# A hybrid decoder step on one core: x handed over turned, block A projected without the tokens' norms, decode work first

## The chip, the core and the metric

The kernel runs on one core of one Trainium2 chip. The metric is the device time of one execution in microseconds (us), the median of several executions. Per-instruction times come from one profiled execution, whose own time stands beside the median below. The core has a matrix engine (PE, with weight loads shown as PEld), a vector engine (DVE), an activation engine (ACT), GpSimd (POOL), and SyncE (SP), which issues most of the DMA transfers.

## What is computed

One layer of a decoder trunk on 1024 prompt tokens and 32 sample tokens (8 sequences of 4), with 2048 features per token:

```python
def mixer_layer(x, pos, conv_buf, attn_fn, norm_in, w_in, g_q, g_k, g_kidx, w_conv, w_out):
    p = split_proj(rmsnorm(x, norm_in) @ w_in)      # 7760 columns
    q = partial_rope(rmsnorm(q, g_q), pos, ROPE_DIM)          # 8 heads x 128
    k = partial_rope(rmsnorm(k, g_k), pos, ROPE_DIM)          # 2 heads x 128
    qi = partial_rope(p["q_idx"], pos, IDX_ROPE_DIM)          # 16 index heads x 64
    ki = partial_rope(rmsnorm(p["k_idx"], g_kidx), ...)       # 64, and 16 head weights w_idx
    attn = attn_fn(q, k, v, qi, ki, wi)    # each query keeps its 256 best keys by
                                           # sum_h w[t,h] relu(q_idx[t,h] . k_idx[s])
    conv, new_buf = short_conv(p["c"] * p["h"], conv_buf, w_conv)
    mix = concat([attn * silu(p["z_attn"]), p["b"] * conv * silu(p["z_conv"])])
    return x + mix @ w_out, k, v, ki, new_buf
```

`rmsnorm(x, g)` divides each token by the root of its mean square and multiplies by `g`. The sample tokens search 8192 cached index keys in pages, and gather the 256 selected rows of the key and value caches. Besides y, the new k, v, index keys and convolution states are returned.

## The kernel before

**Tiling.** The work is cut into block A (prompt tokens 0 to 511 and the 32 sample tokens, 544 columns, kept as two halves of 288 and 256 columns) and block B (prompt tokens 512 to 1023, 512 columns). The projection keeps the features in the partitions: 16 k-tiles of 128 features. For each output tile of 128 columns of `w_in`, `proj` walks over four weight chunks; a chunk is one 256 KB transfer with the weights of four k-tiles (128x512). Both operands are split into a high and a low part: ACT casts `wh` (L494), DVE subtracts to get `wl` (L121, the line of the DVE helper). The same is done for x in `x_part`: ACT writes `xh` (L344), DVE writes `xl`. Each k-tile then costs three matmuls per half (`xh,wh`, `xl,wh`, `xh,wl`, L512).

**Stages.** Each block computes index queries `qi` (8 tiles), index keys `ki` (80 columns), k, v and q (`head_tiles`), the gate z (8 tiles) and the convolution (8 times 4 tiles, `conv_tiles(b, j)`), block A first. The output projections stand at the end. `w` has 4 buffers, `wl` and `wh` 3 each.

**Fillers.** Everything else runs as generators. `slot()`, called after each weight chunk, lets each of four pipes put some instructions into the stream: `main` (index scores and attention of the prompt tiles), `dec` (decode attention), `rms` (the norms of block B) and `vec` (the searches for the 256th best score). Generators in `later` are one-off tails such as `ki_rest`. A scheduler fixes the order of every engine at build; on the chip each engine executes its own list strictly in order. `hp` is the priority that chunk work has over fillers.

**x.** x arrives as rows (tokens in the partitions). `x_load`, `x_rstd` and `x_scale` load the rows, compute each token's factor and scale the rows. PE transposes 128x128 pieces into PSUM (`psx`), and `x_part` splits them from there. Before the first projection, `norm_in`, `w_conv` and `state_conv` are loaded as `rows` and turned by two PE transposes (`pr`). Block B is treated likewise: `x1_load`, `x1_scale` and `prep_x1`, the last of them called after each weight chunk of `conv_tiles(0, 7)`; tiles `xq` hold its rows and come from the pool `g4` of 6 buffers, which also holds the scores `acc` of the prompt search.

**Decode.** `decode_index` gathers index keys of the cache and scores them, `decode_select` searches (with the int16 tile `S`, 128x2304), turns the selection into row numbers (`way`, `pt`, `rid`), and `decode_attend` gathers and attends. In the kernel before `decode_index` and `decode_select` come behind `prompt_index` and `prompt_select` of tiles 2 and 3.

Of the kernel before, what the change touches and what calls it, by code (L numbers as in the profile page):

```python
# [8 lines left out]
F32 = mybir.dt.float32  # L9
# [104 lines left out]
def build(tc, ctx, I, O, stop=None):  # L114
# [86 lines left out]
    def w_out0(ch, c0, m):  # L201
        return I["w_out0"][c0 // 128, :, 4 * ch:4 * ch + 4]

    x_src = [(0, 128, xpr[256:384]), (256, 32, xsa), (128, 128, xpr[384:512]),
             (288, 128, xpr[0:128]), (416, 128, xpr[128:256])]
    x_raw = []

    def x_load(j):

        c0, n, src = x_src[j]  # L210
        if j == 0:
            big = gp.tile([128, 2304], F32, tag="sc", bufs=1, name="xsc")
# [63 lines left out]
    w_d = dp.tile([512], F32, name="w_d", tag="w_d")  # L276

# [57 lines left out]
    rx1 = const((128, 4), "rx1")  # L335

    def x_part(k, ps, xs, hi, lo, a, w):

        for c0, n, parts in xs:
            if a <= c0 < a + w:  # L340
                for a2, w2, t in parts:
                    if a2 <= 128 * k < a2 + w2:
                        transpose(ps[:, c0 - a:c0 - a + n], t[:n, 128 * k - a2:128 * k - a2 + 128], n)
        nc.scalar.activation(out=hi[:, a:a + w], in_=ps[:, :w], func=AF.Copy, scale=norm[:, k:k + 1])  # L344
        stt(lo[:, a:a + w], ps[:, :w], norm[:, k:k + 1], hi[:, a:a + w], MUL, SUB)
# [4 lines left out]
    def x_rstd(js, eng="av"):  # L350

        n = len(js)
        ss = sm((128, 2, n, 2), name="ssx")
        nc.vector.memset(ss, 0.0)
        for c, j in enumerate(js):
            _, rows_, parts = x_raw[j]
            for h, (a, w, t) in enumerate(parts):
                sqx = e2((128, 1024), BF, name="sqx")
                o = ss[:rows_, h % 2, c, h // 2:h // 2 + 1]
                if eng[h % 2] == "a":  # L360
                    nc.scalar.activation(out=sqx[:rows_, :w], in_=t[:rows_, :w], func=AF.Square, accum_out=o)
                else:
                    nc.vector.tensor_tensor_reduce(out=sqx[:rows_, :w], in0=t[:rows_, :w], in1=t[:rows_, :w], scale=1.0,
                                                   scalar=0.0, op0=MUL, op1=ADD, accum_out=o)
        v = sm((128, n), name="vx")
        tt(ss[:, 0], ss[:, 0], ss[:, 1], ADD)
        tt(v, ss[:, 0, :, 0], ss[:, 0, :, 1], ADD)
        ts(v, v, 1.0 / D, EPS, MUL, ADD)
        return rsqrt(v, n, "rx")

    def x_scale(j, h, r, c, eng=None):
        _, n, parts = x_raw[j]
        a, w, t = parts[h]
        if eng is nc.scalar:
            nc.scalar.activation(out=t[:n, :w], in_=t[:n, :w], func=AF.Copy, scale=r[:n, c:c + 1])
        else:
            (eng.tensor_scalar if eng else ts)(t[:n, :w], t[:n, :w], r[:n, c:c + 1], None, MUL)

    def prep_x0():

        x = x_tiles()

        def second():
            yield 1
            yield 1
            x_load(3)
            x_load(4)
            yield 1
            yield 1
            r = x_rstd((3, 4))  # L390
            for _ in range(4):
                yield 1
            for c, j in enumerate((3, 4)):
                for h in range(len(x_raw[j][2])):
                    x_scale(j, h, r, c)
            for _ in range(2):
                yield 1
            for k in range(KT):
                x_part(k, pj(name="psx"), x_raw, *x[k], 288, 256)
                yield 1  # L400
            hp[0] = 200

        r0, r1 = x_rstd((0, 1)), x_rstd((2,))
        for h in range(2):
            x_scale(0, h, r0, 0, nc.scalar)
            x_scale(1, h, r0, 1, nc.scalar)
            x_scale(2, h, r1, 0)
        pr = psm((128, 256), name="pr")
        transpose(pr[:, 0:128], rows[:, 0:128])
# [1209 lines left out]
```

## Time and profile before

| | us |
|---|---|
| median of 3 executions | 2209.12 (2206.09 to 2209.97) |
| the profiled execution | 2209.53 |
| its span, first to last instruction | 2207.6 |
| PE busy | 2162.5 (98%) |
| DVE busy | 1317.3 (60%) |
| ACT busy | 1088.3 (49%) |
| POOL busy | 480.5 (22%) |

Busy time is the union of an engine's instructions. A matmul's record is longer than its distance to the next one, because matmuls overlap in the pipeline; the distance of two starts in the timeline is the better price. The granted clock (PEclk) is 1.00 when PE has its full clock and 0.50 at half.

### The profile page before, as it was taken

What the parts mean: (1) busy time and instruction counts of PE and PEld (TensorE: products, weight loads), DVE (VectorE), ACT (ScalarE), POOL (GpSimd) and SP (SyncE); (2) the same over time, 40 slices, a digit from 0 to 9 for tenths busy, and PEclk for the clock granted to TensorE, in tenths of its full rate; (3) what the DMA queues carried; (4) which work ended last, traced back from release to release, by engine and by line L of the source; (5) the groups of instructions that cost most, each with busy time, mean ns of one, the idle gap of its engine ahead of it and who ended that gap; (6) DMA issues with size and microseconds to landing.
All of it is one profiled execution on the core that took longest, in us unless ns stands there. A gap on an engine that the chain in (4) does not pass through costs nothing.

```text
span 2207.6 us, 37829 instructions
## 1 busy us (share of the span) xinstructions
PE 2162.5 (98%) x13502; PEld 1941.8 (88%) x13502; DVE 1317.3 (60%) x2994; ACT 1088.3 (49%) x2112; POOL 480.5 (22%) x697
## 2 busy tenths in 40 slices
PE   6999999999999999999899999999999999999999
PEld 5899999999999999787688888888888899999887
DVE  6556666555555654799866666556667556443222
ACT  4346666334436566422257684445675565332221
POOL 2111011111113222142531143432331111210000
PEclk9999999999999999999999999999999999999999
DMA  5423444344344333333343344433343384448343
GB/s 195 131 90 117 125 138 135 118 141 131 123 144 140 118 116 104 107 117 113 102 134 117 117 150 129 118 122 105 113 128 113 102 301 117 123 119 275 134 134 110
DMA packets 203720, 290.81 MB, mean 132 GB/s; under 512 B 37588, under 2 KB 87948, under 8 KB 203404
## 3 DMA queue, kind: packets, MB, share of 16 engines
q1 hardware_dynamic: 192268, 254.83, 36.0%
q0 software_dynamic: 11264, 33.57, 5.5%
q8 instruction: 106, 1.74, 0.3%
q14 instruction: 82, 0.67, 0.1%
HBM read 247.53 MB, written 40.78 MB: 131 GB/s over the span
## 4 chain that ended last, share of the span: by engine, by line
PE 50%; DMA 0%; DVE 0%; issue 0%; POOL 0%
PE pj L512 33%; PE po L1503 8%; PE ix L855 1%; PE ix L854 1%; PE pt L174 1%; PE lg L1346 1%; PE dpo L1412 1%; PE kst L174 1%; PE sc L178 1%; PE sc L179 1%; PE po L179 1%; PE po L177 1%; PE po L178 1%; PE sc L177 1%; PE p L174 0%; PE pq L174 0%
## 5 line engine op out<-in xcount | busy, mean ns | idle before, releaser
L512 PE MATMUL pj<-xh,wl 128*128 128x288 f32 (+2 forms) x2800 | 793.0, 329 | 6.9 <-DVE wl L121 6.8
L512 PE MATMUL pj<-xh,wh 128*128 128x288 f32 (+2 forms) x2800 | 791.1, 328 | 6.9 <-DVE xl L121 2.7
L512 PE MATMUL pj<-xl,wh 128*128 128x288 f32 (+2 forms) x2800 | 796.1, 330 | 0.0
L121 DVE TENSOR_TENSOR wl<-w,wh 128x512 fp32r<-128x512 f32 (+1 forms) x613 | 444.1, 726 | 431.2 <-ACT wh L494 397.2
L494 ACT CAST wh<-w 128x512 fp32r<-128x512 f32 x616 | 379.2, 616 | 604.8 <-PE pj L512 380.0
L512 PEld LDWEIGHTS pj<-xh,wh 128*128 128x128 f32 (+1 forms) x2800 | 477.1, 189 | 51.8 <-DVE xl L121 3.1
L512 PEld LDWEIGHTS pj<-xh,wl 128*128 128x128 f32 (+1 forms) x2800 | 474.6, 189 | 51.6 <-DVE wl L121 11.2
L512 PEld LDWEIGHTS pj<-xl,wh 128*128 128x128 f32 (+1 forms) x2800 | 475.1, 189 | 42.2
L886 ACT ACTIVATE junk<-acc,se,se 128x512 int8<-128x512 f32 (+5 forms) x186 | 181.1, 974 | 27.4 <-DVE se L121 24.2
L1096 POOL DMA_INDIRECT G<-in_cache_kidx,gidx x64 | 64.3, 1004 | 388.6 <-PE gd L179 140.4
L121 DVE SCALAR_TENSOR_TENSOR acc<-ixr,wsg,acc 128x512 f32<-128x512 f32 (+3 forms) x150 | 98.3, 668 | 45.9 <-ACT ixr L857 44.7
L857 ACT ACTIVATE ixr<-ix,wab 128x512 f32<-128x512 f32 (+3 forms) x160 | 95.3, 613 | 54.9 <-PE ix L855 53.6
L512 PE MATMUL pj<-mxh,wl 128*128 128x272 f32 x512 | 109.8, 292 | 0.0
L512 PE MATMUL pj<-mxl,wh 128*128 128x272 f32 x512 | 109.4, 291 | 0.0
L512 PE MATMUL pj<-mxh,wh 128*128 128x272 f32 x512 | 108.9, 291 | 0.0
L1392 POOL DMA_INDIRECT Vs<-in_cache_v,rid x64 | 66.4, 1038 | 123.8 <-DVE Vl L121 36.1
L1004 ACT CAST pthl<-pt 128x256 fp32r<-128x256 f32 x144 | 49.6, 371 | 80.6 <-PE pt L174 79.4
L121 DVE TENSOR_TENSOR pthl<-pt,pthl 128x256 fp32r<-128x256 f32 x144 | 57.2, 420 | 50.6 <-ACT pthl L1004 50.0
L512 PEld LDWEIGHTS pj<-mxh,wh 128*128 128x128 f32 x512 | 81.5, 189 | 0.7
L512 PEld LDWEIGHTS pj<-mxl,wh 128*128 128x128 f32 x512 | 81.6, 189 | 0.3
L512 PEld LDWEIGHTS pj<-mxh,wl 128*128 128x128 f32 x512 | 81.3, 189 | 0.4
L990 POOL TENSOR_SCALAR P<-P,l 128x128 f32<-128x128 f32 (+7 forms) x64 | 51.9, 811 | 133.5 <-DVE l L989 102.7
(430 smaller groups left out, 3233.7 us busy)
## 6 DMA issues: line engine op xcount, KB each, us to landing
w<-in_w_in SPq DMA_DIRECT2D x480, 256.0 KB
w<-in_w_out SPq DMA_DIRECT2D x128, 256.0 KB
q_d<-qt SPq DMA_DIRECT2D x72, 64.0 KB
xr<-in_x_a SPq DMA_DIRECT2D x16, 272.0 KB
out_y_a<-xr SPq DMA_DIRECT2D x16, 272.0 KB
xq<-in_x_prompt SPq DMA_DIRECT2D x8, 512.0 KB
xq<-in_x_prompt SPq DMA_DIRECT2D x16, 256.0 KB
q<-q_d SPq DMA_DIRECT2D x32, 128.0 KB
```

Of the source, the lines that this page charges most:

```text
L121: i = f(*a, **k)
L174: nc.tensor.transpose(out, in_, ident[:p, :p])
L177: nc.tensor.matmul(out, lh, rh, start=start, stop=False)
L494: nc.scalar.copy(hi, w)
L512: nc.tensor.matmul(p[:m, :n], w[c][:, k % 4], x[k][b][:, a:a + n], start=(k == 0 and c == b), stop=(k == KT - 1 and c == 1))
L857: nc.scalar.activation(out=r[:, :w], in_=ps[:, :w], func=AF.Relu, scale=wab[:, g, h:h + 1])
L886: nc.scalar.activation(out=junk[:, :n], in_=S, func=AF.Sign, scale=sg, bias=cand, accum_out=s)
L990: nc.gpsimd.tensor_scalar(P[:, :n], P[:, :n], l, 0.5, MUL, MUL)
L1004: nc.scalar.copy(t[:, 0], ptv)
L1096: nc.gpsimd.indirect_dma_start(out=G, out_offset=None, in_=cki, in_offset=bass.IndirectOffsetOnAxis(ap=idx[:, 8 * s + g:8 * s + g + 1], ax ...
L1392: nc.gpsimd.indirect_dma_start(out=W[:, hf], out_offset=None, in_=cv, in_offset=bass.IndirectOffsetOnAxis(ap=rid[:, hf, q:q + 1], axis=0))
L1503: nc.tensor.matmul(ps[i], x[k_][b][:, 128 * i:128 * i + 128], w[c], start=(k_ == 0 and c == b), stop=(k_ == KT - 1 and c == 1))
```

## The change

The host hands x over turned (features in the partitions), as `x_a` and `x_b`, and also `norm_in`, `w_conv` and `state_conv`. `x_part` reads the loaded tile itself; the 144 `psx` and 2 `pr` transposes are gone. The first half of `x_a` is loaded in steps of 1, 1, 1, 1 and then 2 k-tiles, between the weight chunks of the first output tile; the second half in steps of 2 k-tiles per two slots.

Block A is projected from x without the tokens' factors. These come later, from 10 additional loads of the rows (`xt`) with an ACT square each: `rx`, and through DRAM as the rows `R` (factor of each token) and `R2` (its square). They are multiplied in where a result is used: in ki, k, v, the q norm (`mean`, through `ex`), the gate and the convolution (one or two more DVE products per piece). `ki_rest`, `k_rest` and `v_rest` wait with their remaining work for `rx`. Block B is still scaled ahead, but by one `tt` product of a tile with `R1` for each two k-tiles (8 of 128x1024) in place of 16 `ts` products with a column.

Decode goes first in its pipes, its queries are made separately, the last convolution of block A takes its weight columns in pairs (`group` 2), the early `wl` moves from POOL to DVE, and the scaling of the attention weights P by l moves from POOL to ACT. The area for the descriptors of POOL's DMAs is made smaller.

```diff
+        t = g4((128, n, w), name="xs") if n > 1 else g2((128, n, w), name="xs1")
+        nc.sync.dma_start(t, I["x_a"][:, k:k + n, cols])
...
-        nc.scalar.activation(out=hi[:, a:a + w], in_=ps[:, :w], func=AF.Copy, scale=norm[:, k:k + 1])
-        stt(lo[:, a:a + w], ps[:, :w], norm[:, k:k + 1], hi[:, a:a + w], MUL, SUB)
+        nc.scalar.activation(out=hi[:, a:a + w], in_=raw, func=AF.Copy, scale=norm[:, k:k + 1])
+        stt(lo[:, a:a + w], raw, norm[:, k:k + 1], hi[:, a:a + w], MUL, SUB)
...
+        for c in range(4):
+            if c < 3:
+                early.append(load_w(w_in(c, C_QI, 128)))
+            raw = []
+            for n in ((1, 1, 1, 1), (2, 2), (2, 2), (2, 2))[c]:
+                raw += x_load(0, 4 * c + len(raw), n)
+            for k in range(4):
+                put(0, 4 * c + k, raw[k])
...
+                    nc.sync.dma_start(t[rs], src[:, 1024 * h:1024 * h + 1024])
+                    sqx = e2((128, 1024), BF, name="sqx")
+                    nc.scalar.activation(out=sqx[rs], in_=t[rs], func=AF.Square, accum_out=ss[rs, i, h:h + 1])
...
+        while b == 0 and "rx" not in done:
+            yield 1
...
-        for i, (_, _, ((_, _, t),)) in enumerate(parts):
-            ts(t, t, rx1[:, i:i + 1], None, MUL)
+        for t in parts:
+            tt(t, t, R1[0].unsqueeze(1).to_broadcast([128, 2, 512]), MUL)
...
+            for p, c in nat(b, ps):
+                tt(out[:, c], p, R[:, c], MUL)
+            nc.scalar.activation(out=th, in_=out, func=AF.Tanh, scale=0.5)
+            stt(out, th, 1.0, out, ADD, MUL)
...
-        group = 1 if after is None or b == 0 else 2
+        group = 1 if after is None else 2
...
-                nc.scalar.copy(ce[:, c], p)
+                if b == 0:
+                    tt(ce[:, c], p, R2[:, c], MUL)
+                else:
+                    nc.scalar.copy(ce[:, c], p)
...
+            if b == 0:
+                tt(y, y, R, MUL)
...
-            nc.gpsimd.tensor_scalar(P[:, :n], P[:, :n], l, 0.5, MUL, MUL)
+            ts(l, l, 0.5, None, MUL)
+            nc.scalar.activation(out=P[:, :n], in_=P[:, :n], func=AF.Copy, scale=l)
...
-    main.add(prompt_index(2), prompt_index(3), decode_index())
+    main.add(decode_index(), prompt_index(2), prompt_index(3), decode_queries())
     main.add(*(prompt_attend(i) for i in range(4)))
-    vec.add(prompt_select(2), prompt_select(3), decode_select())
+    vec.add(decode_select(), prompt_select(2), prompt_select(3))
...
+    R1.append(g2(name="R1"))
+    nc.sync.dma_start(R1[0], r1_d.rearrange("(o n) -> o n", o=1).to_broadcast([128, 512]))
```

How the instructions stand is shown at three places. **First**, the start of PE's list, before:

```order
L174 MATMUL pr<-ident,rows 128x128 x2
L174 MATMUL psx<-ident,xsc 128x128 x5
L174 MATMUL psx<-ident,xs 128x32 x5
L174 MATMUL psx<-ident,xs 128x128 x5
L512 MATMUL pj<-xh,wh 128x288
L174 MATMUL psx<-ident,xsc 128x128
L174 MATMUL psx<-ident,xs 128x32
L174 MATMUL psx<-ident,xs 128x128
```

and after:

```order
L479 MATMUL pj<-xh,wh 128x288
L479 MATMUL pj<-xl,wh 128x288
L479 MATMUL pj<-xh,wl 128x288
L479 MATMUL pj<-xh,wh 128x288
L479 MATMUL pj<-xl,wh 128x288
L479 MATMUL pj<-xh,wl 128x288
```

The transposes ahead of the first matmuls and between them are gone. **Second**, DVE where block A's convolution ends and block B begins, before (`y` is the product of the last convolution, `xl` the low part of block B's x, `zt` belongs to the attention of a prompt tile, `se` to a search):

```order
L121 TENSOR_TENSOR y<-pj,y 128x288
L121 TENSOR_TENSOR pthl<-pt,pthl 128x256
L121 TENSOR_TENSOR y<-pj,y 128x256
L121 TENSOR_TENSOR wl<-w,wh 128x512
L121 TENSOR_SCALAR se<-tot,se_7576 128x1
L121 SCALAR_TENSOR_TENSOR se_7577<-se,se_7577 128x1
L121 TENSOR_TENSOR zt<-po,zt 128x256
L121 SCALAR_TENSOR_TENSOR xl<-psx,norm,xh 128x512 x3
L121 TENSOR_SCALAR se<-tot,se_7576 128x1
L121 TENSOR_TENSOR wl<-w,wh 128x512
L121 TENSOR_TENSOR wl<-w,wh 128x4x80
```

and after, the last reads of the convolution's PSUM tiles (`cm<-pj,R`) with what follows, and the rows ahead of the first `xl`:

```order
L121 TENSOR_TENSOR cm<-pj,R 128x288
L121 TENSOR_TENSOR cm<-pj,R 128x256
L121 TENSOR_TENSOR pthl<-pt,pthl 128x256
L121 TENSOR_TENSOR wl<-w,wh 128x4x80
L121 TENSOR_TENSOR S<-S 128x2304
...
L121 TENSOR_SCALAR pt_10531<-pg_10528,ptc 128x256
L121 TENSOR_TENSOR pt_10530<-pt_10530,pt_10531 128x256
L121 TENSOR_TENSOR xq_10648<-xq_10648,R_10646 128x1024
L121 TENSOR_TENSOR xq_10650<-xq_10650,R_10646 128x1024
...
L121 TENSOR_TENSOR xq_10658<-xq_10658,R_10646 128x1024
L121 TENSOR_TENSOR pthl<-pt,pthl 128x256
L121 SCALAR_TENSOR_TENSOR xl<-xq_10648,norm,xh 128x512 x2
```

The first `xl` now stands behind decode's work on `S`, behind `pt`, and behind six products of 128x1024. **Third**, DVE during the index queries of block B (`qish`, `qit`), before:

```order
L121 TENSOR_TENSOR wl<-w,wh 128x512
L989 RECIPROCAL l<-l 128x1
L121 TENSOR_SCALAR S<-S 128x2304
L121 TENSOR_SCALAR nm<-mx 128x1
L121 TENSOR_TENSOR wl<-w,wh 128x512
L121 TENSOR_SCALAR S<-S 128x2304
L578 TENSOR_REDUCE kiv<-kisq 128x4
L989 RECIPROCAL l<-l 128x1
L121 TENSOR_TENSOR S<-S 128x2304
L622 STREAM_SHUFFLE qish<-pj 128x512
```

and after:

```order
L600 STREAM_SHUFFLE qish<-pj 128x512
L121 SCALAR_TENSOR_TENSOR ids<-pt_10530,pg_10529 128x256
L121 TENSOR_TENSOR qit<-pj,cosi 128x512
L121 SCALAR_TENSOR_TENSOR ids<-way,ids 128x256
L121 TENSOR_TENSOR wl<-w,wh 128x512 x2
L1266 CAST rid<-pidx 128x64
L121 TENSOR_TENSOR wl<-w,wh 128x512
L121 TENSOR_TENSOR qhl<-pq,qhl 128x256
```

The work on `S` has moved out of this stage, to block A.

## Rows read from the trace of the kernel before

**Rows 1.** page: busy time, share of the span and instructions of each engine.

```profile
PE 2162.5 (98%) x13502; PEld 1941.8 (88%) x13502; DVE 1317.3 (60%) x2994; ACT 1088.3 (49%) x2112; POOL 480.5 (22%) x697
```

**Rows 2.** windows by stage: from:to, length, busy (instructions), PEclk, DMA share, GB/s.

```profile
core 0: us, PE busy (x) PEld busy (x) DVE busy (x) ACT busy (x) POOL busy (x), PEclk, DMA share, GB/s
110.00:878.00 768.00, 768.00 (x5898) 748.35 (x5897) 437.42 (x1071) 411.63 (x815) 140.19 (x215) 1.00 0.40 125
878.00:907.00 29.00, 24.94 (x183) 23.07 (x182) 21.86 (x54) 20.49 (x36) 9.02 (x19) 0.94 0.35 110
955.00:1068.00 113.00, 107.33 (x488) 85.33 (x487) 110.96 (x167) 30.83 (x60) 43.98 (x35) 1.00 0.33 107
1068.00:1103.00 35.00, 27.27 (x127) 21.42 (x126) 25.25 (x72) 8.63 (x16) 17.86 (x26) 0.85 0.37 116
```

**Rows 3.** PE by form, 0 to 110 us: xcount | busy us, mean ns.

```profile
L512 PE MATMUL pj<-xl,wh 128*128 128x288 f32 x128 | 40.8, 322 | 0.0
L512 PE MATMUL pj<-xl,wh 128*80 128x288 f32 x16 | 5.3, 329 | 0.0
L512 PE MATMUL pj<-xl,wh 128*80 128x256 f32 x16 | 4.6, 290 | 0.0
```

**Rows 4.** timeline of PE: start us, us, instruction, [idle before <-releaser].

```profile
11.23 0.66 PE L174 MATMUL pr<-ident,rows 128*128 128x128 f32 x2 [11.23 <-DMA rows<-in_w_conv]
...
21.65 0.61 PE L512 MATMUL pj<-xh,wh 128*128 128x288 f32 x1 [0.24 <-ACT xh L344]
...
23.36 0.44 PE L512 MATMUL pj<-xh,wl 128*128 128x288 f32 x1
23.60 0.44 PE L512 MATMUL pj<-xh,wh 128*128 128x288 f32 x1
...
33.02 0.29 PE L512 MATMUL pj<-xh,wh 128*128 128x288 f32 x1
...
33.29 0.29 PE L512 MATMUL pj<-xh,wl 128*128 128x288 f32 x1
...
904.19 1.57 PE L174 MATMUL psx<-ident,xq 128*128 128x128 f32 x12
906.57 0.46 PE L512 MATMUL pj<-xh,wh 128*80 128x512 f32 x1 [0.81 <-DVE xl L121]
```

**Rows 5.** DMA engines from 0 to 8 us, GB/s in 40 equal slices.

```profile
GB/s 0 0 0 0 0 0 0 0 164 410 0 41 41 287 410 410 369 492 451 369 369 451 492 369 266 430 369 246 123 246 205 184 266 225 225 246 266 287 287 369
```

**Rows 6.** DVE by form, 0 to 110 us.

```profile
L121 DVE SCALAR_TENSOR_TENSOR xl<-psx,norm,xh 128x288 fp32r<-128x288 f32 x16 | 7.4, 512 | 9.5 <-ACT xh L344 9.5
```

**Rows 7.** DVE by form, 955 to 1068 us.

```profile
L121 DVE TENSOR_TENSOR S<-S 128x2304 int16<-128x2304 int16 x16 | 25.4, 1589 | 0.0
L121 DVE TENSOR_SCALAR S<-S 128x2304 int16<-128x2304 int16 x16 | 15.8, 986 | 0.1
L1239 DVE TENSOR_REDUCE way<-S 128x256 f32<-128x2304 int16 x1 | 4.2, 4227 | 0.0
L121 DVE TENSOR_TENSOR pthl<-pt,pthl 128x256 fp32r<-128x256 f32 x10 | 3.8, 414 | 0.0
```

**Rows 8.** timeline of DVE in that stretch.

```profile
993.25 1.35 DVE L121 TENSOR_TENSOR S<-S 128x2304 int16<-128x2304 int16 x1
994.52 0.14 DVE L121 TENSOR_SCALAR nm<-mx 128x1 f32<-128x1 f32 x1
```

**Rows 9.** DVE by form, 878 to 907 us.

```profile
L121 DVE SCALAR_TENSOR_TENSOR xl<-psx,norm,xh 128x512 fp32r<-128x512 f32 x14 | 10.2, 746 | 3.2 <-ACT xh L344 3.0
L121 DVE TENSOR_SCALAR xq<-xq,rx 128x512 f32<-128x512 f32 x4 | 1.8, 482 | 2.6 <-DMA xq<-in_x_prompt 2.6
```

**Rows 10.** page: groups of the whole span.

```profile
L121 DVE TENSOR_TENSOR wl<-w,wh 128x512 fp32r<-128x512 f32 (+1 forms) x613 | 444.1, 726 | 431.2 <-ACT wh L494 397.2
L990 POOL TENSOR_SCALAR P<-P,l 128x128 f32<-128x128 f32 (+7 forms) x64 | 51.9, 811 | 133.5 <-DVE l L989 102.7
```

**Rows 11.** DVE by form, 1068 to 1103 us.

```profile
L121 DVE TENSOR_SCALAR pt<-pg,ptc 128x256 int16<-128x256 int32 x16 | 6.5, 413 | 0.2
```

More of the change, by code (lines that the diff above doesn't have):

```diff
@@ L371, in x_scale, with x_load @@
[L371 to L377, printed above, removed]
+    def x_load(half, k, n):
+        _, w, cols = x_half[half]
+        t = g4((128, n, w), name="xs") if n > 1 else g2((128, n, w), name="xs1")
+        nc.sync.dma_start(t, I["x_a"][:, k:k + n, cols])
+        return [t[:, i] for i in range(n)]
@@ L379, in prep_x0, with put @@
     def prep_x0():
         x = x_tiles()
+        def put(half, k, raw):
+            a, w, _ = x_half[half]
+            x_part(k, raw, *x[k], a, w)
         def second():
-            yield 1
[L385 to L409, printed above, removed]
-        transpose(pr[:, 128:256], rows[:, 128:256])
@@ new lines, in second @@
+            v = sm((128, 5), name="vx")
+            tt(v, ss[:, :, 0], ss[:, :, 1], ADD)
+            ts(v, v, 1.0 / D, EPS, MUL, ADD)
+            ts(ex, v, EPS, None, MUL)
+            nc.vector.tensor_copy(rx, rsqrt(v, 5, "rx"))
+            tt(rx2, rx, rx, MUL)
+            done.add("rx")
+            nc.sync.dma_start(r_d.rearrange("(g p) -> p g", p=128), rx)
+            for a, w, c in ((0, 512, 0), (512, 32, 608)):
+                nc.sync.dma_start(R[:, a:a + w], r_d[c:c + w].rearrange("(o n) -> o n", o=1).to_broadcast([128, w]))
@@ L652, in k_rest @@
         yield from head_tok(b, raw, t, sq, v)
-        ts(v, v, 1.0 / 128, EPS, MUL, ADD)
+        while b == 0 and "rx" not in done:
+            yield 1
+        mean(b, v, 128)
         r = rsqrt(v, nt, "kr")
@@ L1273, in decode_find, with decode_queries @@
         done.add("dsel")
[L1275 to L1276 removed]
+    def decode_queries():
+        while "qn0" not in done:
             yield waiting
[L1278 to L1281 removed]
         qd = const((128, 2, 32, 2, 4), "qd", F32R)
@@ L1286, in decode_attend @@
         zv = [const((128, 2, 144), f"zv{j}", F32R) for j in range(2)]
-        def zeros(ps, start):
-            nc.tensor.matmul(ps, zk[0][:, 0, 0:128], kih[0][:, :ps.shape[1]], start=start, stop=not start)
+        sc["qd"] = qd, zk, zv
         def queries():
@@ L1314, in queries, with decode_attend, zeros @@
             yield 1
-            st["q"] = 1
+            done.add("qd")
+        yield queries()
+    def decode_attend():
+        while not {"dsel", "z0", "qd"} <= done:
+            yield waiting
+        nb, rid = sc["nb"], sc["rid"]
+        qd, zk, zv = sc["qd"]
+        ck = I["cache_k"].rearrange("o n p h d -> (o n p) (h d)")
+        cv = I["cache_v"].rearrange("o n p h d -> (o n p) (h d)")
+        st = {}
+        def zeros(ps, start):
+            nc.tensor.matmul(ps, zk[0][:, 0, 0:128], kih[0][:, :ps.shape[1]], start=start, stop=not start)
         def keys(q):
@@ L1324, in keys @@
             yield 1
-            while "q" not in st or st.get("k") == dec.turn:
+            while st.get("k") == dec.turn:
                 yield 1
```

163 lines of the change are left out of this document (76 added, 87 removed).

## The prediction

> **What bounds the kernel now.** The busy table comes first: PE is busy for 98% of the span and DVE for 60% [rows 1], so time is won only where PE stands still, runs at half clock or does work that the change removes. The windows by stage say where that is [rows 2]. From 110 to 878 us PE is busy for all of 768 us, with DVE at 57%: nothing to win there, and much to lose if DVE gets fuller. Three stages are left. The head: PE first works at 11.23 us and multiplies at 21.65 [rows 4]. The turn from block A to block B, 878 to 907 us: 24.94 busy of 29, clock 0.94. Block B's index and key stage, 955 to 1103 us: from 955 to 1068 DVE is busy for 110.96 of 113 us and PE idles 5.7; from 1068 to 1103 PE idles 7.7 at clock 0.85 [rows 2]. There PE waits for DVE, whose excess is decode's work on S [rows 7].
>
> **Head.** Before, the eight index tiles and ki are done by 110 us: that window holds all their 384 matmuls of 128x288, 48 of 80x288 and 48 of 80x256 (three groups of equal count; one of each is shown) [rows 3]. At full rate two matmuls take 0.27 us from 33.02 to 33.29 [rows 4], 0.135 each, so the work is 51.8 + 6.5 + (at 256/288 of the price) 5.8 = 64 us. The other 46 are the loads ahead of the transposes, the transposes, and a slow start: from 23.36 to 23.60 a matmul took 0.24.
>
> After, there are no transposes. DMA delivers from about 2.6 us on at some 370 GB/s [rows 5]; norm, one k-tile of x (147 KB) and one chunk (256 KB) are 1.1 us of that, then a split of some 1.3 us: first matmul near 5 us. The first output tile is limited from two sides: 48 matmuls at the slow 0.24 are 11.5 us, and DVE must make 16 `xl` of 0.512 [rows 6] and about six `wl` of 0.726 [rows 10], 12.5 us. So it ends near 17.5. Seven tiles at 48 x 0.135 (45.4) and ki (12.2) follow: 75, and 78 with 3 for stalls, since DVE, ACT and DMA all carry the second half of x and the row loads here. 78 against 110 is **-32** (-26 to -37). The 10 row loads (4.46 MB, 12 us of DMA) and the ACT squares lie beside later tiles; if they got in front of the chunks, PE would pay up to 12 us.
>
> **Block B's index stage.** The work on S leaves it (the third place in the order). The idle 5.7 + 7.7 and the half clock, 0.15 x 35 = 5.3, sum to 18.7. The chains of k and v that follow in that stage stay, so I take **-17** (-12 to -19).
>
> **The turn from block A to block B.** This decides. Before, the loss is 4.1 idle, 64 transposes at 1.57/12 = 0.13 [rows 4], some 8 us, and 0.06 x 29 = 1.7 of clock: 14 us. After, the transposes go, but between the last `cm<-pj,R`, which waits for the last convolution matmul, and the first `xl`, without which PE can't pass block B's second matmul, DVE has 88 instructions (the second place). Their sum: 9 products on S at 1.35 (the undisturbed one in [rows 8]; the mean is 1.59), 12.2; 4 `ts` on S at 0.986, 3.9; `way` 4.2; 13 of 128x256 at 0.414, 5.4 [rows 7]; 6 products xq x R1, which before doesn't have, at twice a 128x512 `wl`, 1.45 each, 8.7; 8 of 512 or 544 columns at 0.726, 5.8 [rows 10]; 11 on integers at 0.413, 4.5 [rows 11]; 4 P of 384 columns, not in a row here, at 0.55 as an estimate between the 0.414 of 256 columns and the 0.726 of 512, 2.2; 32 small ones, 5.2. That is 52.1. In [rows 8] the next instruction starts 0.08 before the end of the last, so 88 x 0.08 = 7 come off: 45 us. The price of xq x R1 lies between the 0.482 x 2 of the `ts` it replaces [rows 9] and twice the slowest `wl`; I take the product's row, being a product too.
>
> The Trainium skill ("VectorE: DVE Perf Modes", The perf-mode tier table) speaks against this edit: in fp32 a `tensor_tensor` has no faster mode, where a `tensor_scalar` has one of twice the rate. The trace agrees: `ts` 0.482, product 0.726. By the fixed-latency formula of that page (The TRN2 errata section), an estimate, a 1024-wide product takes 1.22 us; the sum would be 1.4 us smaller.
>
> Beside these 45 us PE has only 25 `po`, 20 transposes, 12 `sc` and one `lg`, near 8 us at the pitch per column above: it stands still for 37. Then come 15 more `xl` at 0.746 [rows 9] with some ten other instructions, 16 us against the 48 ki matmuls' 11.5: 4.5 more. Half clock after the stop: 4, between the 1.7 and the 5.3 of the two stages above. 46 against 14 is **+32** (+22 to +46). The cover is thin: of the four attention rounds in this stretch each needs PE, DVE, ACT and DVE again, in fixed order with S in between, so a round's latency can add to it. The tiles xq also share `g4` with the search's scores, so their loads may start only when the search ends here.
>
> **Block A's convolution.** The rest of the decode tail, some 45 us of DVE, now falls into about six of the last output tiles, 90 us. DVE's share of 0.57 there rises to 1.07: **+6** (0 to +14).
>
> **The rest.** 64 scalings of P go from POOL (51.9 us, [rows 10]) to ACT, which is half idle; the DVE products with R and R2 lie under PE's matmuls in block A; the waits for `rx` concern queued remainders, with k and v behind them. The cover is DVE's 43% of free time from 110 to 878; where it is gone they cost what DVE takes. **+4** (0 to +12). The smaller descriptor area costs nothing while few of POOL's gathers are open at once; if it made them wait, decode, which now has a long lead, is behind.
>
> **Sum.** -32 - 17 + 32 + 6 + 4 = -7. The profiled execution took 2209.53 for a span of 2207.6; the median is 0.4 lower. 2209.1 - 7 = **2202 us**, own range 2190 to 2212.
>
> **Rivals.** (A) The turn is cheap. If xq x R1 costs no more than the `ts` it replaces (3 us less) and ki's `xl` keep up with its matmuls (4.5 less), with 2 us less of half clock, the turn is +22; with the convolution at 0 and the head at -36 that gives 2209 - 36 - 17 + 22 + 0 + 2 = 2180. For it: POOL loses 51.9 us of work [rows 10], and S has a mean of 1.59 but took 1.35 in [rows 8], so something beside DVE slows it. Against: the 88 instructions stand in fixed order, and none can be passed. (B) Slower: the attention rounds at the turn wait for each other. PE waits for P of one round, ACT and DVE for PE; with four rounds at some 4 us of latency beside S the turn loses 62 instead of 46, the convolution 10: 2209 - 32 - 17 + 48 + 10 + 5 = 2223. It is slower than before from a turn that loses 53 us on. For it: before, with a shorter list on DVE at the turn, PE idles for 4.1 us there already [rows 2]. Against: S fills part of the latency. (C) The head gains half, because the small steps of x arrive late or the second half and the rows delay the weight chunks: -18 in place of -32 gives 2216. For it: six ACT squares in a row stand among the casts of the ki chunks. Against: 147 KB steps beside 256 KB chunks, with [rows 5] at 370 GB/s for loads that follow each other.
>
> The Trainium skill ("DMA: Bandwidth & Descriptors", Bandwidth) bears on (C): it wants transfers of 1 MB or more for three quarters of the peak, and lists 138 GB/s at 64 KB. At that rate, an estimate, the first half of x (2.4 MB) would take 17 us, and the first tile would end some 8 us later. No run here shows such small steps alone.
>
> **How the numbers follow.** Forecast 0.42, A 0.23, B 0.22, C 0.13. A measurement of this kernel tells 0.2% (4.4 us) from no change, so faster means below 2204.7 and slower above 2213.5. The forecast's range gives 0.27 faster and 0.13 same, with 0.02 slower; A is all faster; B 0.03 same and 0.19 slower; C 0.03 same and 0.10 slower. Faster 0.50, same 0.19, slower 0.31. The range goes from below A's centre to above B's: 2176 to 2226.
>
> **What would show it.** In the profile after: the first projection matmul near 5 us and ki done near 78; no PE idle of over 2 us between 955 and 1103's counterpart; one idle stretch of PE of 30 us or more between block A's last convolution and block B's ki, with DVE full and the granted clock at half behind it; DVE over 95% in the last convolution tiles of block A. Idle of under 20 us at the turn would prove me wrong towards A. Idle with DVE itself waiting for PE or ACT would be B, and PE waiting for DMA or `wh` ahead of 80 us would be C.

## The result and the profile after

The changed kernel takes 2220.63 us (median of 8 runs, 2218.31 to 2226.77), the kernel before 2207.47 (8 runs, 2205.86 to 2212.57). The ratio is 1.0058, 95% interval 1.0048 to 1.0069: slower by 0.58%. Forecast were 2202 us and a gain. The profiled execution has a span of 2218.3 us against 2207.6, so 10.7 us have to be found.

The page of the kernel after, busy time of each engine (it answers to [rows 1]), and its windows by stage (it answers to [rows 2]; columns as there):

```profile
PE 2148.5 (97%) x13356; PEld 1929.2 (87%) x13356; DVE 1315.1 (59%) x3044; ACT 1126.5 (51%) x2148; POOL 423.4 (19%) x630
```

```profile
core 0: us, PE busy (x) PEld busy (x) DVE busy (x) ACT busy (x) POOL busy (x), PEclk, DMA share, GB/s
20.00:40.00 20.00, 15.17 (x106) 13.93 (x104) 15.98 (x36) 10.62 (x23) 5.26 (x6) 1.00 1.00 351
...
88.00:200.00 112.00, 103.89 (x779) 100.37 (x777) 59.98 (x151) 45.45 (x94) 26.77 (x31) 0.95 0.41 119
200.00:400.00 200.00, 200.00 (x1474) 190.46 (x1473) 105.61 (x174) 80.83 (x151) 35.35 (x36) 1.00 0.41 127
...
780.00:880.00 100.00, 92.77 (x713) 91.19 (x711) 87.99 (x208) 45.67 (x103) 23.61 (x32) 0.97 0.32 92
880.00:940.00 60.00, 24.94 (x82) 16.69 (x83) 53.39 (x105) 18.32 (x39) 11.46 (x18) 0.57 0.22 67
940.00:1120.00 180.00, 178.68 (x873) 145.79 (x872) 106.84 (x241) 66.79 (x132) 75.41 (x97) 1.00 0.42 130
```

Read the PE column against the length of each window. From 200 to 780 us PE never stops, as before. In three windows it does: 88 to 200 (8.1 us idle, clock 0.95), 780 to 880 (7.2 idle, 0.97) and 880 to 940 (35 idle, 0.57). The first two had no counterpart before, where PE was busy for all of 110 to 878.

Its groups of waits of PE (waited for: us in total, times, longest) name what ended each stop:

```profile
PE pt L174 <- ACT P L991: 16.7, 4, 7.3
PE sc L177 <- DVE qhl L121: 8.2, 1, 8.2
PE pp L1057 <- DVE pt L1055: 8.1, 1, 8.1
PE po L178 <- DVE pthl L121: 8.1, 4, 5.8
PE pj L479 <- ACT wh L461: 7.4, 3, 5.7
PE pj L479 <- DVE wl L121: 5.0, 5, 2.0
```

Rows two, four and most of row one (14.5 of 16.7) belong to the turn. Row three is the new stop near 110 us. There the timelines of the DMA queue on SP, of DVE and of PE (start, us, instruction, [idle before <-releaser]) read:

```profile
98.05 0.51 SPq L378 DMA_DIRECT2D r_d<-rx  x1
98.72 0.41 SPq L565 DMA_DIRECT2D w_d<-wd  x1
106.49 0.79 SPq L380 DMA_DIRECT2D R<-r_d  x2
107.33 0.38 SPq L1054 DMA_DIRECT2D pt8i<-in_page_table  x1
107.81 0.34 SPq L460 DMA_DIRECT2D w<-in_w_in  x1
...
101.23 0.36 DVE L570 COPY kit<-kit 128x320 f32<-128x320 f32 x1
111.48 0.73 DVE L121 TENSOR_TENSOR R<-R 128x544 f32<-128x544 f32 x1 [9.89 <-DMA R<-r_d]
112.39 0.18 DVE L1055 CAST pt<-pt8i 8x64 f32<-8x64 int32 x1 [0.19 <-DMA pt8i<-in_page_table]
112.50 0.69 DVE L121 TENSOR_TENSOR wl<-w,wh 128x512 fp32r<-128x512 f32 x1
...
104.22 0.29 PE L479 MATMUL pj<-xl,wh 128*128 128x288 f32 x1
112.63 0.68 PE L1057 MATMUL pp<-pt,dc 8*128 8x64 f32 x2 [8.11 <-DVE pt L1055]
...
113.62 0.66 PE L479 MATMUL pj<-xh,wl 128*128 128x288 f32 x2
...
117.98 0.41 PE L479 MATMUL pj<-xh,wh 128*128 128x288 f32 x2
```

The norms are written to DRAM at 98.05, and the read of R, which needs that write, is issued at 106.49: 8.4 us for 2.5 KB, which by the code are 640 single elements of 4 bytes. Apart from the write of `wd` at 98.72, SP issues nothing in between; for 7.3 us of it the trace books its wait to the write of the norms. The page table and the next weight chunk stand behind the read. R lands at 111.48, 13.4 us after the write was issued. DVE stands at R x R for 9.89 us, and `pt` and the next `wl` stand behind it in DVE's order. PE runs out at 104.5 and is idle 8.11 us; then two matmuls take 0.45 from start to start (113.62 to 114.07 in the same view) where later they take 0.25, until 117.98. The releaser named, `pt`, is the last link only.

The turn, in the timelines of SP, DVE and PE of the kernel after:

```profile
919.17 0.37 SPq L1554 DMA_DIRECT2D R<-r_d  x1
...
878.78 0.78 DVE L121 TENSOR_TENSOR cm<-pj,R 128x288 f32<-128x288 f32 x2
...
910.66 4.04 DVE L1240 TENSOR_REDUCE way<-S 128x256 f32<-128x2304 int16 x1
...
922.62 5.04 DVE L121 TENSOR_TENSOR xq<-xq,R 128x1024 f32<-128x1024 f32 x4
...
928.32 2.40 DVE L121 TENSOR_TENSOR xq<-xq,R 128x1024 f32<-128x1024 f32 x2
...
930.98 1.49 DVE L121 SCALAR_TENSOR_TENSOR xl<-xq,norm,xh 128x512 fp32r<-128x512 f32 x2
...
894.78 0.69 PE L177 MATMUL sc<-kth,qhl 128*128 128x384 f32 x1 [8.24 <-DVE qhl L121]
...
904.81 0.98 PE L174 MATMUL pt<-ident,P 128*128 128x128 f32 x2 [7.31 <-ACT P L991]
...
918.60 1.27 PE L174 MATMUL pt<-ident,P 128*128 128x128 f32 x4 [7.23 <-ACT P L991]
...
931.11 0.58 PE L178 MATMUL po<-pthl,vh 128*128 128x256 f32 x1 [5.75 <-DVE pthl L121]
```

From the start of the last two `cm` to the first `xl` DVE takes 52.2 us, as the order of the instructions had said; PE gets a short piece of attention every 8 us or so. What the order did not say is in the first row: R1, the broadcast of the second half's norms, is read at 919.17, though the norms were written at 784.99 (SP's row `r_d<-rx` L419).

**Where the 10.7 us come from**, idle and half clock by stage: head -27 (below), stop near 110 +11 (8.1 idle, and 5.4 us of work at half clock, from 112.6 to 118.0, which costs some 2.5), end of block A's convolution +10 (7.2 idle, and 5.7 us of work at half clock, from 818.4 to 824.1, which costs some 2.6), turn +31 (35 idle and some 20 us of work at half clock, 45, against 14 before), index and key stage -15 (1.3 idle against 16 before, see below). Sum +10. The clock of a window can't be multiplied by its length here: the granted clock also stands at 0.50 from 108 to 112 us, where PE does nothing, so 0.05 x 112 would count idle time twice.

### The profile page after: what moved, and what is told of

It is laid out like the page before. It is cut to its first block, busy times and chain, and to the rows that moved or that the text cites. A ratio compares the mean times of both kernels' runs of the same rounds, so it can differ in the third digit from the quotient of the medians.

```text
span 2218.3 us, 37535 instructions
## 1 busy us (share of the span) xinstructions
PE 2148.5 (97%) x13356; PEld 1929.2 (87%) x13356; DVE 1315.1 (59%) x3044; ACT 1126.5 (51%) x2148; POOL 423.4 (19%) x630
## 5 line engine op out<-in xcount | busy, mean ns | idle before, releaser
L479 PE MATMUL pj<-xh,wh 128*128 128x288 f32 (+3 forms) x2800 | 787.2, 328 | 8.6 <-ACT wh L461 7.4
L479 PE MATMUL pj<-xl,wh 128*128 128x288 f32 (+3 forms) x2800 | 791.3, 329 | 0.0
L121 DVE TENSOR_TENSOR wl<-w,wh 128x512 fp32r<-128x512 f32 x616 | 440.4, 716 | 414.6 <-ACT wh L461 361.2
L886 ACT ACTIVATE junk<-acc,se,se 128x384 int8<-128x384 f32 (+5 forms) x186 | 181.1, 974 | 23.3 <-DVE se L121 19.0
L958 POOL TENSOR_TENSOR q<-q,ssq 128x256 f32<-128x256 f32 x32 | 22.2, 693 | 512.5 <-DMA q<-q_d 260.6
L1018 POOL TENSOR_TENSOR zt<-zt 128x256 fp32r<-128x256 f32 x32 | 28.5, 890 | 324.3 <-ACT zt L1017 321.6
L121 DVE SCALAR_TENSOR_TENSOR rl<-gd,rh 128x512 fp32r<-128x512 f32 x64 | 44.1, 690 | 71.2 <-ACT rh L1114 70.9
L1114 ACT ACTIVATE rh<-gd 128x512 fp32r<-128x512 f32 x64 | 38.3, 599 | 87.6 <-PE gd L179 87.2
```

The source lines that it names most:

```text
L121: i = f(*a, **k)
L479: nc.tensor.matmul(p[:m, :n], w[c][:, k % 4], x[k][b][:, a:a + n], start=(k == 0 and c == b), stop=(k == KT - 1 and c == 1))
L886: nc.scalar.activation(out=junk[:, :n], in_=S, func=AF.Sign, scale=sg, bias=cand, accum_out=s)
L958: nc.gpsimd.tensor_tensor(q4, q4, rq[:, 2 * hp:2 * hp + 2].unsqueeze(2).to_broadcast([128, 2, 128]), MUL)
L1018: nc.gpsimd.tensor_tensor(zt.bitcast(F32R), zt, hi, SUB)
L1114: nc.scalar.activation(out=rh, in_=ps, func=AF.Relu)
```

## The experiments

The first four were made together; each later one rests on those ahead of it. "After" stands for the changed kernel; each ratio is to the kernel before on the same chip, with its 95% interval.

**1. R's read and its square leave SP and DVE.** The theory was that the stop near 110 is SP's and DVE's wait for R; the rival was that the page table is late in any case.

```diff
-                nc.sync.dma_start(R[:, a:a + w], r_d[c:c + w]...
+                nc.gpsimd.dma_start(R[:, a:a + w], r_d[c:c + w]...
-            tt(R2, R, R, MUL)
+            nc.gpsimd.tensor_tensor(R2, R, R, MUL)
```

> The changed kernel with one edit: the two reads of R from DRAM are issued by POOL instead of SP, and R2 = R x R is computed by POOL instead of DVE. Theory (the round trip blocks two queues): after the 2.5 KB write of rx SP waits 8 us before it can issue the read of R, with the page table's load and a weight chunk behind it, and DVE waits 9.9 us for R with the next wl behind it. PE then idles 8.1 us and runs the next 11 us at half clock. Without it 12 to 14 us less than the changed kernel's 2220.6: 2206 to 2209. Rival (the page table itself): the matmul on it would be late anyway, so at least 4 us of idle and the half clock stay: 2212 to 2216. Rival (given back): block A's later stages are bound by DVE, so the time is lost again before the turn to block B: 2218 to 2221.

2220.57 us, ratio 1.0056 [1.0039, 1.0073]: no gain. DVE, in the timeline of this run, no longer waits for R but for the page table, which SP issued at 102.67, right behind the two writes:

```profile
113.72 0.18 DVE L1055 CAST pt<-pt8i 8x64 f32<-8x64 int32 x1 [8.54 <-DMA pt8i<-in_page_table]
```

It landed 11 us after its issue. The stop has more than one cause in series, and this edit took away one.

**2. The old order of decode and prompt.** If decode first is what makes the turn dear, the old order with all other edits should win.

```diff
-    main.add(decode_index(), prompt_index(2), prompt_index(3), decode_queries())
+    main.add(prompt_index(2), prompt_index(3), decode_index(), decode_queries())
-    vec.add(decode_select(), prompt_select(2), prompt_select(3))
+    vec.add(prompt_select(2), prompt_select(3), decode_select())
```

> The changed kernel with one edit: the prompt tiles 2 and 3 come ahead of decode in the pipes again (index and search), as in the kernel before. Theory (the turn from block A to block B is bound by decode's work on S in DVE's list): PE's loss at the turn falls from 45 us to about 12, the 10 us in block A's last convolution tiles go too, and block B's index and key stage loses its 18 us again: 2220.6 - 33 - 10 + 18 = 2196, between 2190 and 2202. Rival (the turn is bound by R1's round trip and the late loads of xq): the turn keeps 30 us or more and the index stage loses 18 in addition: 2225 to 2240.

2234.79 us, ratio 1.0122 [1.0105, 1.0139]: 14 us slower than after, against the expectation. Its windows:

```profile
870.00:950.00 80.00, 68.50 (x345) 54.87 (x344) 63.56 (x130) 44.28 (x78) 16.84 (x24) 0.91 0.36 112
...
1040.00:1110.00 70.00, 47.64 (x203) 37.31 (x202) 57.56 (x122) 14.35 (x26) 19.12 (x26) 0.83 0.28 85
...
2020.00:2080.00 60.00, 45.97 (x208) 36.94 (x207) 17.41 (x42) 16.41 (x32) 1.47 (x2) 0.86 0.53 174
```

The turn is cheaper (after has 44.56 busy of the same 80), but PE idles 22.4 us in the key stage, where after has 70.00 busy of 70, and 14 us in the output projection, into which more of the attention of the prompt tiles has slipped (32 transposes of P from 2000 to 2100 us, 17 in after; after is 59.36 busy of 60). Decode's own attention ends near 1530 us. Decode first costs at one place and pays at two.

**3. P times 1/l back on POOL.**

```diff
-            ts(l, l, 0.5, None, MUL)
-            nc.scalar.activation(out=P[:, :n], in_=P[:, :n], func=AF.Copy, scale=l)
+            nc.gpsimd.tensor_scalar(P[:, :n], P[:, :n], l, 0.5, MUL, MUL)
```

> The changed kernel with one edit: P is scaled by l on POOL again instead of ACT. Theory (PE's 16.7 us of waits for P at ACT are a wait for what stands ahead on DVE): the time stays at 2220.6, within 5 us, and the waits are now booked to POOL. Rival (ACT is the bound there): 8 to 12 us less, 2209 to 2213.

2223.04 us, ratio 1.0074 [1.0057, 1.0091], 2.4 us above after with overlapping intervals: the move to ACT is at most a small gain, and the waits of PE for P at the turn stay (16.5 us). They are not the price of ACT.

**4. An eighth of the row loads.** This leaves out seven eighths of the sums of squares, with their loads.

```diff
-                    nc.sync.dma_start(t[rs], src[:, 1024 * h:1024 * h + 1024])
+                    nc.sync.dma_start(t[rs, :128], src[:, 1024 * h:1024 * h + 128])
...
-                    nc.scalar.activation(out=sqx[rs], in_=t[rs], ...
+                    nc.scalar.activation(out=sqx[rs, :128], in_=t[rs, :128], ...
```

> The changed kernel with the row loads and their squares cut to an eighth (128 of each 1024 columns; this leaves out seven eighths of the sums of squares of block A). Theory (the row loads stand ahead of weight chunks while DMA is full from 20 to 46 us): PE's loss from 20 to 60 us, about 7.5 us, falls to 3 or less, so 4 to 6 us less: 2214 to 2217. Rival (the head is bound by DVE's xl and wl and by the slow rate of the first tile): 2219 to 2222.

2216.76 us, ratio 1.0040 [1.0026, 1.0054]: about 4 us less than after by the medians, with intervals that still overlap; its profiled execution, the slowest of its five, had the same span, 2218.3. In that trace PE idles 4.5 us from 20 to 60, in after 6.4: the stop of 1.20 us for `wh` is gone, but the two longest, 2.04 and 1.82 us for `wl` on DVE, are in both. So the rows cost the head some 2 us by the trace (the window 20 to 40 of after has DMA at 1.00); whether 4, as the medians have it, is not shown. The stop near 110 stays, at 8.6 us.

**5 and 6. The page table early; then with R on POOL too.** Number 5 loads `pt8i` at the head of the program, into a tile of its own; number 6 adds the lines of number 1.

```diff
+    pt8i = const((8, 64), "pt8i", I32)
...
+            nc.sync.dma_start(pt8i..., I["page_table"]...)
             hp[0] = 200
...
-            nc.sync.dma_start(pt8i..., I["page_table"]...)
```

> The changed kernel with one edit: the page table (2 KB, 512 single elements) is loaded ahead of the row loads, into a tile of its own, instead of behind the reads of R. Theory (two waits of DVE in a row, for R and for the page table, each alone long enough to starve PE): DVE still waits some 10 us for R with wl behind it, PE still idles 6 to 8 us near 110: 2217 to 2221. Rival (the page table alone): PE's stop near 110 goes, 2206 to 2210.

2220.70 us, ratio 1.0056 [1.0039, 1.0073]. The stop moves: PE passes `pp` and stands 4.91 us for `kil`, which is behind R x R on DVE.

```diff
-                nc.sync.dma_start(R[:, a:a + w], r_d[c:c + w]...
+                nc.gpsimd.dma_start(R[:, a:a + w], r_d[c:c + w]...
```

> The changed kernel with both edits: the page table early, and R read and squared by POOL. Theory (two waits in a row): with both gone PE does not stop near 110, its 6 to 8 us and the half clock behind them are back, 10 to 14 us in all: 2206 to 2211. Rival (given back at the turn, where DVE is the bound): 2217 to 2221.

2220.24 us, ratio 1.0048 [1.0032, 1.0065]. It moves again, to decode's first gather, as the timelines of POOL and PE show:

```profile
111.22 1.32 POOL L382 DMA_DIRECT2D R<-r_d  x2 [31.25 <-DMA r_d<-rx]
116.78 1.09 POOL L384 TENSOR_TENSOR R<-R 128x544 f32<-128x544 f32 x1 [4.24 <-DMA R<-r_d]
118.03 1.05 POOL L1098 DMA_INDIRECT G<-in_cache_kidx,gidx  x1 [0.16 <-issue]
...
121.47 1.12 PE L174 MATMUL gt<-ident,G 128*128 128x128 f32 x4 [7.71 <-DMA G<-in_cache_kidx,gidx]
```

Whichever queue carries the read of R stands until the write has landed, and on each something was due.

**7. A buffer of its own for R1.** At the turn R1 takes a buffer of the shared pool `g2`. If that is why its read comes at 919.17, a tile of its own brings it forward, and the turn becomes cheap though decode stays first.

```diff
-    R1.append(g2(name="R1"))
+    R1.append(const((128, 512), "R1"))
```

> The changed kernel with one edit: R1, the row of block B's token factors, has a tile of its own instead of one of ten shared buffers. In the changed kernel its read from DRAM waits for a DVE instruction that frees a buffer and is issued at 919 us, though the factors are written at 785 and five of the six first xq were asked for long before. Theory (the missing buffer, not decode first, puts the products xq x R1 behind the work on S): the first xl stand ahead of most of the work on S, PE's loss at the turn falls from 45 to 12 to 18 us, block B's index stage loses 5 to 15 again, and SP waits 6 to 8 us for the write of the factors near 785, which costs 0 to 6: 2197 to 2212. Rival (DVE has too much to do there in any order): PE's loss moves into the last convolution tiles and the index stage, 2216 to 2222.

2211.16 us, ratio 1.0007 [0.9997, 1.0016]: 9.5 us better than after (by the ratios 11). Its SP queue and DVE near 800 us, and its windows at the turn and behind it:

```profile
789.70 0.39 SPq L419 DMA_DIRECT2D r_d<-rx  x1
798.62 0.33 SPq L1554 DMA_DIRECT2D R<-r_d  x1
...
802.57 5.77 DVE L121 TENSOR_TENSOR xq<-xq,R 128x1024 f32<-128x1024 f32 x5 [7.49 <-DMA R<-r_d]
...
869.36 0.74 DVE L121 SCALAR_TENSOR_TENSOR xl<-xq,norm,xh 128x512 fp32r<-128x512 f32 x1
```

```profile
870.00:950.00 80.00, 76.11 (x398) 62.52 (x397) 79.36 (x144) 34.87 (x70) 23.55 (x24) 0.98 0.40 125
950.00:1110.00 160.00, 148.66 (x698) 120.65 (x696) 98.37 (x240) 57.45 (x119) 67.54 (x97) 0.93 0.37 113
```

Number 6, which turns as after does, has 43.89 busy of 80 at clock 0.70 in the same first window and 160.00 of 160 in the second. So the turn's loss was R1's late read: with R1 at hand `xl` stands among the work on S and not behind it. Two things are given back: DVE waits 7.49 for R1's own trip through DRAM, which, with the five products behind it, stops PE for 7.79 us at 808.73, and the second window loses 11 us.

**8. Numbers 6 and 7 together, R1 read by POOL as well.**

```diff
-    nc.sync.dma_start(R1[0], r1_d...
+    nc.gpsimd.dma_start(R1[0], r1_d...
```

> The changed kernel with the edits of e6_pt_R and e7_r1_own, and R1 read by POOL too. Theory (three causes that add up): 12 us below e7_r1_own, 2186 to 2200, so 0.3% to 1% faster than the kernel before. Rival (the gains overlap, since DVE bounds block A's end): 2203 to 2212.

2207.97 us, ratio 0.9995 [0.9985, 1.0004]: the rival's figure, no gain over the kernel before. The two trips still show as 7.00 us at 121.01 (`gt`, for G) and 10.90 at 808.65 (for `u`, behind xq x R1 on DVE). A change of queue does not shorten a trip: from the write of the norms to R x R it took 14.3 us in number 1 and 16.7 in number 6, against 13.4 in after.

**9. No trip at all.** R and R1 are spread on the core: DVE copies each column of norms across 128 columns, PE transposes it, ACT copies it out of PSUM. R1 has its own tile, and the page table is early (its lines are those of number 5).

```diff
+    def spread(out, col, n, a, w):
+        wide = g2(name="wide")
+        nc.vector.tensor_copy(wide[:, :128 * n]..., col[:, :n].unsqueeze(2).to_broadcast([128, n, 128]))
+        ps = psb(name="spread")
+        for g in range(n):
+            transpose(ps[:, 128 * g:128 * g + 128], wide[:, 128 * g:128 * g + 128])
+        nc.scalar.copy(out[:, :w], ps[:, a:a + w])
...
-            nc.sync.dma_start(r_d.rearrange("(g p) -> p g", p=128), rx)
-            for a, w, c in ((0, 512, 0), (512, 32, 608)):
-                nc.sync.dma_start(R[:, a:a + w], r_d[c:c + w]...
+            spread(R, rx, 4, 0, 512)
+            yield 1
+            spread(R[:, 512:544], rx[:, 4:5], 1, 96, 32)
...
-                nc.sync.dma_start(r1_d.rearrange("(g p) -> p g", p=128), rx1)
+                R1.append(const((128, 512), "R1"))
+                spread(R1[0], rx1, 4, 0, 512)
...
-    R1.append(g2(name="R1"))
-    nc.sync.dma_start(R1[0], r1_d...
```

> The changed kernel, with the page table early, and R and R1 made on the core instead of through DRAM: DVE copies each factor along a row, PE transposes it (five and four transposes), ACT copies it out of PSUM; R1 has a tile of its own. Theory (the round trips through DRAM, of 640 and 512 single elements each, are what DVE, SP and POOL wait for near 110 and 808 us): both stops go, 8 us idle and 5 of half clock near 110, 11 idle and 5 of half clock near 808, against e8_all's 2207.97: 2182 to 2194, so 0.7 to 1.2% faster than the kernel before. Rival (behind each of them stands another late step, such as the first gather of index keys or the products xq x R1): 2198 to 2207.

2192.83 us (2190.09 to 2195.59), ratio 0.9919 [0.9900, 0.9939]: faster than both kernels. Its answer on the tile `spread` (count, min/median/max ns, first and last start) and its windows:

```profile
L174 PE MATMUL spread<-ident,wide x9: 270/272/273, 102.9 to 780.9; 128*128 128x128 f32 x9
L326 ACT COPY R<-spread x3: 191/587/587, 105.8 to 781.3; 128x512 f32<-128x512 f32 x2, 128x32 f32<-128x32 f32 x1
...
88.00:130.00 42.00, 42.00 (x338) 41.62 (x338) 25.46 (x84) 21.09 (x45) 4.96 (x5) 1.00 0.42 123
...
870.00:950.00 80.00, 77.74 (x351) 60.28 (x350) 75.84 (x138) 28.23 (x61) 27.49 (x28) 1.00 0.41 127
950.00:1110.00 160.00, 143.97 (x687) 115.63 (x686) 95.95 (x241) 61.27 (x126) 66.70 (x101) 0.94 0.38 114
```

Nine transposes, three copies on DVE and three on ACT replace two trips of 13 us; the stop near 110 is gone to the last tenth, and PE, DVE and ACT take it beside other work. The last window is the price: it is 143.97 busy of 160, where number 6, with the dear turn, has 160.00.

**10. The same, with the page table where the change has it.** This tells whether the table was a cause by itself; the edit is against number 9.

```diff
-    pt8i = const((8, 64), "pt8i", I32)
+            pt8i, pt8 = sm((8, 64), I32, name="pt8i"), sm((8, 64), name="pt8")
```

> As e9_pe_R, but with the page table loaded where the changed kernel loads it. Theory (without the writes of the factors in the DMA queues the page table lands some 2 to 4 us after its issue and hurts little): within 5 us of e9_pe_R. Rival (512 single elements take 5 us or more by themselves and PE waits for them): 5 to 12 us above e9_pe_R.

2194.51 us, ratio 0.9931 [0.9908, 0.9954], not to be told from number 9. The table is issued at 101.86 and in use at 106.06, with no wait for it: it was late only where it stood behind the write of the norms.

**11. R alone spread on the core**, R1 as in after. It divides the gain between the two causes; the edit is against number 10.

```diff
-                R1.append(const((128, 512), "R1"))
-                spread(R1[0], rx1, 4, 0, 512)
+                nc.sync.dma_start(r1_d.rearrange("(g p) -> p g", p=128), rx1)
...
+    R1.append(g2(name="R1"))
+    nc.sync.dma_start(R1[0], r1_d...
```

> The changed kernel with R alone made by PE's transposes; R1 stays in its shared buffer and goes through DRAM. Theory (two separate causes, the stop near 110 us and the turn to block B): only the stop near 110 goes, 8 us idle and 5 of half clock, and the turn's 45 us stay: 2206 to 2211. Rival (DVE bounds block A's end, so that without R1's buffer the gain is given back at the turn): 2217 to 2222.

2210.69 us, ratio 1.0014 [1.0005, 1.0024]. So R's trip was worth 10 us of after, and R1 (trip and late buffer) another 16 down to number 10 (by the ratios 18). PE's waits at the turn are as after's (8.2 for `qhl`, 15.3 for P, where after has 8.2 and 16.7).

**12. Number 10 with the old order.** Number 2 said that the old order is dearer; does that hold with R and R1 mended?

```diff
-    main.add(decode_index(), prompt_index(2), prompt_index(3), decode_queries())
+    main.add(prompt_index(2), prompt_index(3), decode_index(), decode_queries())
-    vec.add(decode_select(), prompt_select(2), prompt_select(3))
+    vec.add(prompt_select(2), prompt_select(3), decode_select())
```

> e10_pe_R_nopt with prompt tiles 2 and 3 ahead of decode in the pipes again. Theory (decode last is worse because its tail falls into block B's index stage and attention is left for the output projection, whatever the factors do): 10 to 18 us above e10_pe_R_nopt, 2204 to 2213. Rival (decode first costs more than it brings, and e2_order was slow because of the round trips): 2185 to 2197.

2220.57 us, ratio 1.0053 [1.0036, 1.0070]: 26 us above number 10, more than expected. Its windows:

```profile
870.00:950.00 80.00, 80.00 (x380) 65.07 (x379) 49.26 (x113) 40.52 (x71) 24.20 (x34) 1.00 0.40 127
950.00:1040.00 90.00, 76.91 (x351) 61.40 (x349) 77.71 (x137) 29.17 (x60) 24.97 (x27) 0.90 0.30 94
1040.00:1110.00 70.00, 41.47 (x174) 32.61 (x175) 55.58 (x118) 12.43 (x22) 17.80 (x27) 0.74 0.23 67
...
2000.00:2100.00 100.00, 91.73 (x480) 78.13 (x480) 33.52 (x67) 27.46 (x51) 1.46 (x2) 0.97 0.57 187
```

The turn is without loss, but the two windows behind it lose 41.6 us of PE (16.1 in number 10), the longest stop 13.82 us for `kit` on DVE, where S stands; the output projection loses 8 more. Decode first is worth its place.

## Why the prediction was wrong

The forecast had the wrong sign; 2220.63 lies inside its range only because rival B had drawn the upper end out to 2226.

- **The step that failed: "The rest."** It gave +4 to the waits for `rx`, on the ground that they "concern queued remainders", and took DVE's 43% of free time as their cover. The +4 was for other things as well, and none of them shows. The wait itself cost 11 us in after's profile, and taking the trip away gave back 10 (number 11). Free time on DVE is no cover for a wait in DVE's fixed order, with `pt` and `wl` behind it, nor on SP's, with a weight chunk behind it. I had not named what stands behind R x R and behind the read of R, nor priced the write of 640 elements: no row of the trace of before showed one, so a bound from both sides was due, and there was none. This term alone doesn't restore the gain: number 11, without R's trip, is at 1.0014 [1.0005, 1.0024]. The rest of the miss is in the next two terms.
- **Head, predicted -32, measured -27.** First matmul at 5.69 us (near 5 expected). By 86.2 us, where ki is read out, PE has done 397 matmuls of 128x288 where 384 were due (133, 132 and 132 against 128 each), so 13 and as many of 128x256 belong to k: 26 x 0.13 = 3.4, and ki ends at 82.8 for 78. The missing 5 us lie mostly in 20 to 40 us, where DMA is full and PE is 15.17 busy of 20. The 3 us for stalls were too few: PE waits 5.0 us for `wl` on DVE, which has the `xl` of the second half ahead of it, and 1.7 for `wh`. Only the wait for `wh` is rival C's mechanism; all told the rows cost the head some 2 us by number 4's trace.
- **End of block A's convolution, predicted +6, measured +10.** DVE is at 0.88 there, not over 0.95 as I had said it would show; the longest stops there are attention's, 2.87 us for `q` from POOL and 1.44 for P from ACT (timeline of PE at 818.37 and 803.53), not DVE's queue. So the size was near and the reason wrong; no run took these stops away.
- **Turn, predicted +32, measured +31.** The size was right by its own working: 52.2 us from the last `cm` to the first `xl`, of which DVE waited 6.4 (six waits, the longest 2.00 for `ptci`), so 45.8 of work for the 45 of the sum. That PE's loss came out at 45 as well is partly luck: half clock cost 10 where I had 4, and the 4.5 for ki's `xl` do not show, since PE idles less than 0.1 us from 932 to 945. Six products xq x R1 took 5.04 + 2.40 = 7.4 us where I had 8.7. The Trainium skill ("VectorE: DVE Perf Modes", The TRN2 errata section) had it nearer with its formula, 1.22 each; the traces give a median of 1.218. What was wrong is the reason. I took the order in which S stands ahead of xq x R1 as the result of decode first. Numbers 7 and 9 keep decode first and have PE 76 and 78 busy of 80 at the turn: the order came from R1's read, held up by a shared buffer. Not all of the loss can be had back in this way: in number 9 PE idles 34 us less than in number 6 at the turn (77.74 busy against 43.89) and 16 us more in the window behind it. On balance R1's late read and its trip were worth the 16 to 18 us between numbers 11 and 10, not the 31.
- **Index and key stage, predicted -17, measured -15.** PE is 178.68 busy of 180 where it lost 16 before. The 18.7 of the sum took the half clock as 0.15 x 35, which counts the time in which PE stood still; in the trace of before PE works for some 5 us of the stretch at half clock (1077 to 1088), which costs 2.6. Numbers 2 and 12 show the other side: with decode second the loss is back, and larger. But decode first by itself doesn't save it: number 9 keeps that order and idles 16.0 us from 950 to 1110, where the kernel before idles 13.4. With decode first, the runs with the dear turn (after, numbers 6 and 11) idle less than 1 us from 950 to 1110, and those with a cheap turn (7, 8 and 9) 11 to 16 us. The sum had added the two terms as if each stood alone.
- **Rivals.** A is out: 35 us of idle at the turn in after. B had the sign but not the mechanism: the rounds wait for each other a little (6.4 us of DVE), the turn loses 45 and not 62, and the kernel is slower through the stop near 110, for which no rival stood.

What stays open: why the windows from 950 to 1110 lose 16 us in number 9 while after loses next to nothing there. The longest stops are for P, 2.64 and 3.21 us, and for Ks, 2.19; no run took these away. Decode's `way` and all 16 `pt` stand in these windows in number 9, where after has `way` and nine of the `pt` ahead of them; that this is the cause is not shown. Open is also why number 12 idles 41.6 us there, where the kernel before, with decode in the same place, idles 13.4.

## What to carry to other kernels

A value that takes a trip through DRAM to be broadcast is priced by its whole time, here 13 us, and every queue that issues or reads it is searched for what stands behind: moved to another queue it stops something else, and on the core it cost nine transposes and six copies. Where the order on an engine looks dear, ask first what fixed it; a tile that is needed early and takes its buffer late from a shared pool may be the reason. A loss that a reordering brings at one place has to be weighed with what it saves elsewhere, by undoing it alone and again once the other causes are gone; a loss in one stage and a gain in the next need not be two separate terms. The mean clock of a window is no price where PE stands still in it.

## What was not expected of the hardware

A write of 2.5 KB in 640 elements, from its issue to the issue of the read that waits for it, took 8.4 us in after (98.05 to 106.49) and 8.1 in number 5 (102.11 to 110.24); 2 KB in 512 elements took 8.9 (number 7, 789.70 to 798.62). Where POOL issued the read, it came 9.9 us (number 1, 101.64 to 111.54) and 11.2 us (number 6, 100.05 to 111.22) after the write. The read of R behind it took 5.0 more in after (106.49 to 111.48). A page table of 2 KB took 11 us when it was issued right behind these writes (number 1), but 5.1 when it was issued after they had landed (after, 107.33 to 112.39), and at most 4.2 without the write of the norms (number 10, 101.86 to 106.06).
